# 128-column products set between longer ones, x put into PSUM ahead of the last product, and a new draw of the planner

## The chip, the cores and the metric

The kernel runs on one core of a Trainium2 chip. The time is device microseconds of that core for one execution of the whole block; the median of three runs before the change is 423.39 us (423.36 to 423.80). A profile of one execution stands beside it. The engines are named as in the profile: PE is TensorE (PEld its weight loads), DVE VectorE, ACT ScalarE, POOL GpSimd, SP the engine that issues most DMAs.

## The reference

One pre-norm residual layer over 512 tokens of width 1024, with two attention branches fed by one input projection. Its core, cut:

```python
h = rmsnorm(x, norm_g)
(q_lat, c_kv, k_rope, z_a, q_b, k_b, v_b, z_b,
 q_idx, k_idx, w_idx, gate_a, gate_b) = split(h @ w_in)
q  = rmsnorm(q_lat, g_q_lat) @ w_uq      # 8 heads of 64 + 32 (the 32 rotated)
kv = rmsnorm(c_kv, g_kv_lat) @ w_ukv     # 8 heads of 64 keys, 64 values
y_a = softmax_chunk_causal(q, k) @ v * silu(z_a)
# branch b: an indexer scores keys, each query keeps its top 128
y_b = softmax_topk(q_b k_b / 8 + rel_bias) @ v_b * silu(z_b)
merged = sigmoid(gate_a) * (y_a @ w_o_a) + sigmoid(gate_b) * (y_b @ w_o_b)
out = rmsnorm(x + merged @ w_out, final_g)
```

## The kernel before, in words

Nearly all of the work is matrix products. Each operand is kept as a rounded part ("hi", made by an ACT cast) and a remainder ("lo", made by a subtraction on DVE or POOL), and a product is summed in PSUM from two or three single products: hi*hi, hi*lo, lo*hi (`mm3`, `mm`, line 418). Tokens are four tiles of 128.

Order. Nothing is scheduled by the compiler: generators ("threads") yield steps, and a planner (`Flow.run`) keeps a clock for each engine, picks the step that can start first by its table of durations (with a random addition for each thread, from `random.Random(DRAW)`), and emits it. What it emits is the order of instructions on each engine's queue, and each engine runs its queue strictly in that order. `step` durations are the planner's own numbers, written in the code.

Logits. Each MLA head (`mla_head`) makes for token tile i a tile of logits of 128 (i + 1) columns, three products each (lines 1582 to 1584); each DSA head (`dsa_head`) two products each, through `mm`. `ORDER` lists the tiles, 0 to 3, each in its own PSUM bank. DVE takes a row maximum, ACT the exponential, the probabilities are normalised and turned by PE (line 435).

Attention outputs. `attend` multiplies values by the turned probabilities of the key tiles 0 to 3, of 512, 384, 256 and 128 columns, hi and lo, into one bank.

The loads of weights go through four raw buffers by `fetcher` on the SP queue. `PASSED` names four of them whose DMA is issued only after 2 or 6 later DMAs of that queue; one lo part of the DSA values is likewise emitted later than planned (`passed_by`).

The end (`output`). The output product is made of seven block products (numbers 1 to 7) with shared sums. Products 1, 7, 2, 6 and 5 come first; product 5 leaves its result in the banks z (one of 512 columns for the first tile, two of 256 for the second). Product 4 completes columns 0 to 511 of tiles 2 and 3, and product 3 adds to the banks z to complete columns 512 to 1023 of tiles 0 and 1. `finish` halves the bank and adds x on DVE (xr, line 357), takes the sum of squares (ACT Square, or for the very last piece a DVE reduction, line 1861) and multiplies by the gain into rg (line 357). `scale_out` adds the sums, takes the power on POOL (line 396), scales rg on DVE (line 376) or ACT (line 329) and stores it: seven DMAs on SP (line 458), one on ACT (line 1905).

Of the kernel before, what the change touches and what calls it, by code (L numbers as in the profile page):

```python
# [15 lines left out]
ALU = mybir.AluOpType  # L16
# [3 lines left out]
P = 128  # L20
# [243 lines left out]
DRAW = 53  # L264
# [6 lines left out]
def tile_block(ctx: ExitStack, tc: tile.TileContext, a: dict, out: bass.AP, bias_dram: bass.AP):  # L271
# [158 lines left out]
    def turn(parts):  # L430


        def emit():
            for d, s in parts:
                nc.tensor.transpose(d.ap, s.ap, ident.tile)  # L435

        return pe(0.107 * len(parts), [d for d, _ in parts], [s for _, s in parts] + [ident.all], emit, len(parts))

    held = []

    def hold(n, emit):

        return lambda: held.append([n, emit])

    def passed():
        for x in list(held):
            x[0] -= 1
            if not x[0]:
                held.remove(x)
                x[1]()  # L450

    def dma(dst, src):
# [5 lines left out]
        return Step([("SP", n / 360000.0, lambda: (nc.sync.dma_start(d, s), passed()))], bufs(dst), bufs(src))  # L458
# [494 lines left out]
    def fetcher():  # L953
        yield is_done("loads")
        for n, job in enumerate(jobs):
# [144 lines left out]
    passed_by = []  # L1100

    def seven(times, part, c11, c21, c12, c22, end):
# [11 lines left out]
        def add(dst, ps, y):  # L1114
            step = tt(dst, part(ps), y, ALU.add)
            return step.then(lambda: [passed_by.pop()() for _ in list(passed_by)])
# [32 lines left out]
    def values2():  # L1149
# [69 lines left out]
        def take(half, out):  # L1219
            v = yield Get(VV)  # L1220
            for u in range(2):
# [4 lines left out]
                step = lo_part(lo, src, hi)  # L1226
# [3 lines left out]
                yield step  # L1230
# [235 lines left out]
    def attend(br, h, probs, ready, prio):  # L1466
# [29 lines left out]
        for kt, pt, src, dst in ((0, 0, slice(0, S), slice(0, S)), (1, 1, slice(P, S), slice(P, S)),  # L1496
                                 (2, 2, slice(256, S), slice(256, S)), (3, 2, slice(P, 256), slice(384, S))):
            hi, lo = turned[pt]
            yield mm(ps[:, dst], [(v4[:, kt, :], hi[:, src]), (v4[:, kt, :], lo[:, src])], kt == 0, kt == 3)
            if kt != 2:  # L1500
                put(hi, lo)
# [51 lines left out]

    def mla_head(h):
# [7 lines left out]
        def soft(i, ps):  # L1562
            n = P * (i + 1)
            mx = yield Get(SMALL)
            yield Step([("DVE", 0.07 + 0.00104 * n, lambda: nc.vector.tensor_reduce(  # L1565
                mx.tile[:, 1:2], ps.tile[:, :n], op=ALU.max, axis=AX.X, negate=True))], [mx], [ps])
            den = yield from sums[i].at(i)
            yield act(probs[i], ps[:, :n], AF.Exp, bias=mx[:, 1:2], scale=1.0, accum=den)
            put(ps, mx)
            yield from sums[i].normalise(i, probs[i])  # L1570
            ready.add(i)

        for i in ORDER:
            nn = P * (i + 1)
            ps = yield bank("lg")

            def emit():
                o = ps.tile[:, :nn]
                q0, q1 = qh.tile[:, TOK[i]], ql.tile[:, TOK[i]]
                k0, k1 = kh.tile[:, :nn], kl.tile[:, :nn]  # L1580

                nc.tensor.matmul(o, q0[0:100], k0[0:100], start=True, stop=False)  # L1582
                nc.tensor.matmul(o, q0[0:96], k1[0:96], start=False, stop=False)  # L1583
                nc.tensor.matmul(o, q1[0:96], k0[0:96], start=False, stop=True)  # L1584

            yield pe(3 * (0.0133 + nn / 2400), [ps.all], [qh.all, ql.all, kh.all, kl.all], emit, 3)
            spawn(soft(i, ps), prio)
# [62 lines left out]
    def dsa_head(h):  # L1650
# [7 lines left out]
        def soft(i, ps):  # L1658
            n = P * (i + 1)
# [508 lines left out]
```

## Time and profile before

| what | value |
|---|---|
| median of three runs | 423.39 us |
| lowest, highest run | 423.36, 423.80 us |
| span of the profiled execution (first to last instruction) | 421.2 us |
| median less span | 2.19 us |
| granted TensorE clock, mean | 0.995 |
| PE, PEld busy | 413.7 us (98%), 364.3 us (86%) |
| DVE, ACT, POOL busy | 372.8 us (89%), 265.6 us (63%), 125.2 us (30%) |
| mean DMA rate | 156 GB/s |

The page lists no time of the profiled execution other than its span; the median less the span is what lies around the first and last instruction, as far as one execution and a median can be set against each other. A busy PE is not a PE at its peak, since ends of products are modelled; starts of products, starts of weight loads and the idle time before them tell more. Start and length of a row in the timeline are in us from the start of the span; "x7" merges seven instructions.

### The profile page before, as it was taken

The page shows a single profiled execution, that of the slowest core. Times are in us where ns is not written, and L with a number is a line of the kernel's source. Part 1 is how long each engine was busy: PE and PEld are TensorE (multiplying, and loading weights), DVE is VectorE, ACT ScalarE, POOL GpSimd, SP SyncE. Part 2 cuts the span into 40 slices and gives each one's busy share as a digit, 9 for nine tenths or more (in the row PEclk, how much of TensorE's full clock was granted, in tenths as well). Part 3 has the DMA queues.
Part 4 walks back from the last instruction along what each step waited for, and adds up shares of the span by engine and source line. Part 5 has one row for each costly group of instructions (what it writes and reads, how often), then busy time and mean ns, then how long its engine had stood idle before and what let it go on. Part 6 is the DMA issues. An engine that isn't in the chain of part 4 may idle for free.

```text
span 421.2 us, 7078 instructions
## 1 busy us (share of the span) xinstructions
PE 413.7 (98%) x2314; PEld 364.3 (86%) x2314; DVE 372.8 (89%) x797; ACT 265.6 (63%) x596; POOL 125.2 (30%) x139
## 2 busy tenths in 40 slices
PE   8999999999999999999999999999999999999994
PEld 7999878888888888888999988998998888888883
DVE  4879889569999999999999999979799768999995
ACT  5877778586754748625578677694597444336624
POOL 0047768543464669400012000200100000120652
PEclk9999999999999999999999999999999999999998
DMA  7992135665266441444652347144542887248305
GB/s 258 382 337 77 48 94 191 172 206 127 75 156 184 89 151 51 119 146 149 151 163 75 110 142 188 56 166 129 153 138 68 292 296 242 102 148 305 123 1 199
DMA packets 30645, 65.89 MB, mean 156 GB/s; under 512 B 4776, under 2 KB 6200, under 8 KB 30608
## 3 DMA queue, kind: packets, MB, share of 16 engines
q1 hardware_dynamic: 28256, 61.66, 47.4%
q10 hardware_dynamic: 1584, 2.62, 1.7%
q0 software_dynamic: 768, 1.15, 0.9%
q8 instruction: 18, 0.29, 0.3%
q14 instruction: 19, 0.16, 0.1%
HBM read 50.49 MB, written 4.21 MB: 130 GB/s over the span
## 4 chain that ended last, share of the span: by engine, by line
PE 96%; DVE 1%; DMA 1%; issue 0%; POOL 0%; ACT 0%; POOLq 0%; SPq 0%; ACTq 0%
PE ps L418 86%; PE ps L435 5%; PE ps L1583 1%; PE ps L1584 1%; PE ps L1582 1%; PE ps L883 1%; DMA normg<-norm_g 1%; DVE s_xr L357 1%; POOL sm L396 0%; DVE s_rg L357 0%; DVE s_rg L376 0%; ACT s_rg L329 0%; POOLq L2164 0%; ACT s_xg L329 0%; PE ps L932 0%
## 5 line engine op out<-in xcount | busy, mean ns | idle before, releaser
L418 PE MATMUL ps<-s_h,s_w 128*128 128x512 f32 (+1 forms) x732 | 169.9, 379 | 0.0
L418 PEld LDWEIGHTS ps<-s_h,s_w 128*128 128x128 f32 x732 | 128.3, 189 | 22.0
L320 ACT CAST s_w<-raw 128x512 fp32r<-128x512 f32 (+3 forms) x124 | 71.8, 593 | 18.8 <-DMA raw<-w_o 9.3
L348 POOL TENSOR_TENSOR s_w<-raw,s_w 128x512 fp32r<-128x512 f32 (+2 forms) x39 | 48.5, 1255 | 48.1 <-ACT s_w L320 44.2
L346 DVE TENSOR_TENSOR s_w<-raw,s_w 128x512 fp32r<-128x512 f32 (+2 forms) x85 | 55.7, 668 | 4.7 <-ACT s_w L320 3.7
L418 PE MATMUL ps<-s_ys,s_w 128*128 128x512 f32 x192 | 43.8, 389 | 0.0
L418 PEld LDWEIGHTS ps<-s_ys,s_w 128*128 128x128 f32 x192 | 36.0, 188 | 7.5
L329 ACT ACTIVATE s_p<-s_p,sm 128x128 f32<-128x128 f32 (+3 forms) x62 | 32.7, 550 | 5.0 <-DVE sm L1662 4.3
L418 PE MATMUL ps<-s_wo,s_mg 128*128 128x512 f32 (+1 forms) x156 | 33.2, 373 | 0.0
L418 PE MATMUL ps<-s_w,s_xg 128*128 128x328 f32 (+1 forms) x192 | 32.5, 323 | 0.0
L418 PEld LDWEIGHTS ps<-s_wo,s_mg 128*128 128x128 f32 x156 | 27.6, 188 | 5.2
L418 PEld LDWEIGHTS ps<-s_w,s_xg 128*128 128x128 f32 x192 | 31.4, 188 | 0.0
L346 DVE TENSOR_TENSOR s_ph<-ps,s_ph 128x384 fp32r<-128x384 f32 (+1 forms) x48 | 27.6, 593 | 1.0 <-ACT s_ph L320 0.7
L320 ACT CAST s_ph<-ps 128x384 fp32r<-128x384 f32 (+1 forms) x48 | 23.4, 515 | 6.4 <-PE ps L435 5.0
L329 ACT ACTIVATE s_p<-ps,sm 128x128 f32<-128x128 f32 (+3 forms) x32 | 16.8, 527 | 15.7 <-DVE sm L1565 15.6
L348 POOL TENSOR_TENSOR s_p<-s_bias,mask 128x128 f32<-128x128 f32 (+2 forms) x5 | 4.2, 854 | 74.0 <-DMA s_bias<-bias_scratch 39.6
L905 DVE MAX8 sm<-mask 128x8 f32<-128x384 f32 (+2 forms) x48 | 25.7, 549 | 0.2
L906 DVE MATCH_REPLACE8 mask<-sm,mask 128x384 f32<-128x384 f32 (+2 forms) x48 | 25.9, 541 | 0.0
L418 PE MATMUL ps<-s_ph,vv 128*128 128x512 f32 (+3 forms) x128 | 25.1, 318 | 0.0
L435 PE MATMUL ps<-ident,s_p 128*128 128x128 f32 x160 | 23.1, 273 | 0.0
L418 PEld LDWEIGHTS ps<-s_ph,vv 128*128 128x128 f32 x128 | 21.0, 188 | 2.4
L348 POOL TENSOR_TENSOR s_wo<-raw,s_wo 128x512 fp32r<-128x512 f32 x3 | 13.2, 4420 | 28.3 <-ACT s_wo L320 28.3
(194 smaller groups left out, 769.6 us busy)
## 6 DMA issues: line engine op xcount, KB each, us to landing
raw<-w_out SPq DMA_DIRECT2D x18, 512.0 KB, 3.3
s_op<-s_op SPq DMA_DIRECT2D x36, 128.0 KB, 2.3
raw<-w_ga SPq DMA_DIRECT2D x8, 512.0 KB
raw<-w_gb SPq DMA_DIRECT2D x8, 512.0 KB
raw<-w_o SPq DMA_DIRECT2D x16, 256.0 KB, 4.2
s_xn<-x SPq DMA_DIRECT2D x8, 256.0 KB, 4.8
bias_scratch<-s_sig ACTq DMA_DIRECT2D x8, 256.0 KB, 3.0
raw<-w_za SPq DMA_DIRECT2D x4, 512.0 KB, 4.7
```

What stands on the lines that cost most here:

```text
L320: nc.scalar.copy(dst.ap, src.ap)
L329: nc.scalar.activation(dst.ap, src.ap, func, **kw)
L346: opts.append(("DVE", 0.07 + 0.00104 * x.n, lambda: nc.vector.tensor_tensor(dst.ap, x.ap, y.ap, op=op)))
L348: opts.append(("POOL", 0.15 + 0.0021 * x.n, lambda: nc.gpsimd.tensor_tensor(dst.ap, x.ap, y.ap, op=op)))
L357: lambda: nc.vector.scalar_tensor_tensor(dst.ap, x.ap, sc(s), y.ap, op0=op0, op1=op1))],
L418: nc.tensor.matmul(ps.ap, l.ap, r.ap, start=start and i == 0, stop=stop and i == len(pairs) - 1, skip_group_check=more)
L435: nc.tensor.transpose(d.ap, s.ap, ident.tile)
L883: yield pe(0.005 + n / 2400, [ps.all], [qs[h].all, ks[0].all], lambda: nc.tensor.matmul(ps.tile[:, :n], qs[h].tile[:96, TOK[i]], ks[0].til ...
L905: yield Step([("DVE", t, lambda: nc.vector.max(m8.tile, work.tile))], [m8], [work])
L906: yield Step([("DVE", t, lambda: nc.vector.match_replace(work.tile, m8.tile, work.tile, MARK))], [work], [m8])
L1582: nc.tensor.matmul(o, q0[0:100], k0[0:100], start=True, stop=False)
L1583: nc.tensor.matmul(o, q0[0:96], k1[0:96], start=False, stop=False)
```

## The change

It has five parts. `ORDER` now groups token tiles: tiles 2 and 0 of a head share a PSUM bank (384 + 128 columns), and `logits` emits, for each of the two or three single products, first the one of 384 and then the one of 128 columns. `attend` puts the key tiles 1 (384 columns) and 3 (128) in one step, in turn, and leaves key tile 2 for last. The planner's duration of a product of 128 columns is 0.11 us behind another such, and by its columns otherwise (`spans`); a turn is 0.109 in place of 0.107. At the end, `add_first` adds 2x into the banks z on DVE before product 3, so that `finish_twice` squares (ACT) and scales (DVE) straight from PSUM; product 4 runs tile by tile; the outputs may be scaled on either engine, and the sums of squares have a buffer each. Last, `DRAW` is 64, and `PASSED` and `passed_by` are gone.

```diff
-DRAW = 53
+DRAW = 64
...
+    def spans(columns):
+        t, before = 0.0, S
+        for n in columns:
+            t += 0.11 if n <= P and before <= P else 0.0133 + n / 2400
+            before = n
+        return t
...
-        return pe(0.107 * len(parts), ...
+        return pe(0.109 * len(parts), ...
-    held = []
...
-            if n in PASSED:
-                step.options = [("SP", step.options[0][1], hold(PASSED[n], step.options[0][2]))]
...
-                if half == 1 and u == 0:
-                    step.options = [(e, t, lambda emit=emit: passed_by.append(emit)) for e, t, emit in step.options]
...
-        for kt, pt, src, dst in ((0, 0, slice(0, S), slice(0, S)), (1, 1, slice(P, S), slice(P, S)),
-                                 (2, 2, slice(256, S), slice(256, S)), (3, 2, slice(P, 256), slice(384, S))):
-            hi, lo = turned[pt]
-            yield mm(ps[:, dst], [(v4[:, kt, :], hi[:, src]), (v4[:, kt, :], lo[:, src])], kt == 0, kt == 3)
+        for kts in ((0,), (1, 3), (2,)):
+            seq = []
+            for c in range(2):
+                for kt in kts:
+                    pt, src, dst = parts[kt]
+                    seq.append((ps[:, dst], v4[:, kt, :], turned[pt][c][:, src]))
...
+    def logits(ps, rows, parts):
+        seq = []
+        for n, (q, k) in enumerate(parts):
+            for i in rows:
+                seq.append((logits_of(ps, rows, i), q(i), k(P * (i + 1)), n == 0 and i == rows[0], n == len(parts) - 1))
...
-        for i in ORDER:
+        for rows in ORDER:
             ps = yield bank("lg")
-            yield mm(ps[:, :nn], [(qb[:, TOK[i]], kh[:, :nn]), (qb[:, TOK[i]], kl[:, :nn])], True, True)
-            spawn(soft(i, ps), prio)
+            yield logits(ps, rows, [(lambda i: qb[:, TOK[i]], lambda nn, k=k: k[:, :nn]) for k in (kh, kl)])
+            release = shared(ps, rows)
+            for i in rows:
+                spawn(soft(i, logits_of(ps, rows, i), release), prio)
...
+    def add_first(t, half, c0, c1, ps):
+        r = xr[t, half].all.f[:, c0:c1]
+        yield stt(ps[:, c0:c1], r, 2.0, ps[:, c0:c1], ALU.mult, ALU.add)
+        done.add(("added", t, half, c0))
+    def finish_twice(t, half, c0, c1, ps, nth):
+        r = ps[:, c0:c1]
+        spawn(square(t, r, nth, 0.5), PSQUARE)
+        if (t, half) not in rg:
+            rg[t, half] = yield slot("rg")
+        yield stt(rg[t, half].all.f[:, c0:c1], r, 0.5 * D ** 0.5, fg[half].all.f[:, c0:c1], ALU.mult, ALU.mult)
+        done.add(("g", t, nth))
+        yield is_done(("sq", t, nth))
+        put(ps)
...
-        for half, engs in ((0, ("ACT",) if t == 0 else ("DVE",)), (1, ("ACT",))):
+        spawn(half_out(0, ("DVE",)), 0)
+        spawn(half_out(1, ("ACT",) if t == 1 else ("ACT", "DVE")), 0)
...
-        yield from product(4, v, left2, 256)
+        for i in range(2):
+            v.append((yield bank("o")))
+            for k in range(4):
+                yield mm3(v[i].all, cut(left2[k], ...), whole(right[4, k]), k == 0, k == 3)
...
-                yield is_done(("read", 2 + i, 1 + (c0 > 0)), ("sum", i, 1))
+                yield is_done(("added", i, 1, c0))
...
-ORDER = [0,1,2,3]
+ORDER = ((2, 0), (1,), (3,))
-PASSED = {7: 2, 8: 2, 9: 2, 10: 6}
```

How the instructions move. On PE, in the logits of one MLA head, before (qhi is the rounded query, s_op the other operands, ps the bank):

```order
L1582 MATMUL ps_98<-s_op_1286,qhi_74 128x128
L1583 MATMUL ps_98<-s_op_1310,qhi_74 128x128
L1584 MATMUL ps_98<-s_op_1286,s_op_1280 128x128
L1582 MATMUL ps_93<-s_op_1286,qhi_74 128x256
L1583 MATMUL ps_93<-s_op_1310,qhi_74 128x256
L1584 MATMUL ps_93<-s_op_1286,s_op_1280 128x256
```

and of the same head in the changed kernel:

```order
L1572 MATMUL ps_97<-s_op_1287,qhi_74 128x384
L1572 MATMUL ps_97<-s_op_1287,qhi_74 128x128
L1572 MATMUL ps_97<-s_op_1317,qhi_74 128x384
L1572 MATMUL ps_97<-s_op_1317,qhi_74 128x128
L1572 MATMUL ps_97<-s_op_1287,s_op_1278 128x384
L1572 MATMUL ps_97<-s_op_1287,s_op_1278 128x128
```

The three products of 128 columns stood in a row and now stand one by one behind those of 384. In the whole program 74 products other than turns have 128 columns; 41 of them followed another short one before, and 1 does now.

At the end, on DVE, the last rows before (s_xr is x plus what is summed so far, s_rg the output tile, sm and ssf the sums of squares; the brackets name whose work a row waits for):

```order
L357 SCALAR_TENSOR_TENSOR s_xr_4520<-ps_98,s_xr_4520 128x256 [waits PE_49]
L1861 ISA junk,sm_90<-s_xr_4520,sm_90 128x256 [waits DVE_49]
L1861 ISA sm_90 128x1
L357 SCALAR_TENSOR_TENSOR s_rg_4837<-s_xr_4520,s_fg_4538 128x256
L376 TENSOR_SCALAR s_rg_4664<-s_rg_4664,sm_90 128x512 [waits Pool_49]
```

and now:

```order
L357 SCALAR_TENSOR_TENSOR s_rg_4828<-ps_98,s_fg_4591 128x512 [waits Activation_49]
L376 TENSOR_SCALAR s_rg_4769<-s_rg_4769,sm_81 128x512
L365 TENSOR_SCALAR sm_89<-ssf_128,sm_89 128x1
L357 SCALAR_TENSOR_TENSOR s_rg_4848<-ps_92,s_fg_4591 128x256 [waits Activation_49]
L376 TENSOR_SCALAR s_rg_4664<-s_rg_4664,sm_89 128x512 [waits Pool_49]
L365 TENSOR_SCALAR sm_91<-ssf_130,ssf_131 128x1
L357 SCALAR_TENSOR_TENSOR s_rg_4848<-ps_94,s_fg_4591 128x256 [waits Activation_49]
L365 TENSOR_SCALAR sm_91<-ssf_132,sm_91 128x1 [waits DVE_49]
L376 TENSOR_SCALAR s_rg_4671<-s_rg_4671,sm_91 128x512 [waits Pool_49]
```

The addition of x and the DVE reduction are gone from the last piece; the gain is multiplied straight from the bank, and that row waits for ACT.

On ACT, the last rows of the changed kernel (ps_98 is tile 0, ps_92 and ps_94 are the halves of tile 1; sm_89 belongs to tile 0, sm_91 to tile 1):

```order
L329 ACTIVATE junk,ssf_128<-ps_98 128x512 [waits PE_49,Activation_49]
L329 ACTIVATE junk,ssf_131<-ps_92 128x256 [waits PE_49,Activation_49]
L329 ACTIVATE s_rg_4828<-s_rg_4828,sm_89 128x512 [waits Pool_49]
L329 ACTIVATE junk,ssf_132<-ps_94 128x256 [waits PE_49,Activation_49]
L329 ACTIVATE s_rg_4848<-s_rg_4848,sm_91 128x512 [waits Pool_49]
```

Three squares now read PSUM, and the scaling of tile 0 stands ahead of the last square.

More of the change, by code (lines that the diff above doesn't have):

```diff
@@ L435, in emit @@
                 nc.tensor.transpose(d.ap, s.ap, ident.tile)
-        return pe(0.107 * len(parts), [d for d, _ in parts], [s for _, s in parts] + [ident.all], emit, len(parts))
-    held = []
[L441 to L450, printed above, removed]
+        return pe(0.109 * len(parts), [d for d, _ in parts], [s for _, s in parts] + [ident.all], emit, len(parts))
     def dma(dst, src):
@@ L457, in dma @@
             n *= x
[L458 removed]
+        return Step([("SP", n / 360000.0, lambda: nc.sync.dma_start(d, s))], bufs(dst), bufs(src))
     def pool_dma(dst, src):
@@ L954, in fetcher @@
         yield is_done("loads")
-        for n, job in enumerate(jobs):
+        for job in jobs:
             raw = yield Get(RAW)
@@ L1114, in add @@
         def add(dst, ps, y):
-            step = tt(dst, part(ps), y, ALU.add)
-            return step.then(lambda: [passed_by.pop()() for _ in list(passed_by)])
+            return tt(dst, part(ps), y, ALU.add)
         x = yield bank("mm")
@@ L1552, in prob_tiles, with logits_of, shared, release @@
         return s, [v[0][:, 0:128], v[1][:, 0:256], v[0][:, 128:512], v[2]]
+    def logits_of(ps, rows, i):
+        c = sum(P * (r + 1) for r in rows if r < i)
+        return ps[:, c : c + P * (i + 1)]
+    def shared(ps, rows):
+        left = [len(rows)]
+        def release():
+            left[0] -= 1
+            if not left[0]:
+                put(ps)
+        return release
+    def logits(ps, rows, parts):
[3 more added lines that the diff above has]
+                seq.append((logits_of(ps, rows, i), q(i), k(P * (i + 1)), n == 0 and i == rows[0], n == len(parts) - 1))
+        def emit():
+            for o, q, k, start, stop in seq:
+                nc.tensor.matmul(o.ap, q.ap, k.ap, start=start, stop=stop, skip_group_check=len(rows) > 1)
+        return pe(spans(k.n for _, _, k, _, _ in seq), [ps.all],
+                  [v for _, q, k, _, _ in seq for v in (q, k)], emit, len(seq))
     def mla_head(h):
@@ L1845, in final_loads, with finish @@
         done.add("final")
-    ssf = [fixed(f"ssf{t}", [P, 4]) for t in range(NT)]
+    ssf = [[fixed(f"ssf{t}{n}", [P, 1]) for n in range(3)] for t in range(NT)]
     rg = {}
-    def finish(t, half, c0, c1, ps, nth, last, keep=False):
+    def finish(t, half, c0, c1, ps, nth, keep=False):
         r = xr[t, half].all.f[:, c0:c1]
@@ L1857, in finish @@
         done.add(("read", t, nth))
-        if last:
-            yield Until(lambda: t in partial_sum)
-            s = partial_sum[t]
-            step = Step([("DVE", 0.1 + 0.00104 * r.n, lambda: nc.vector.tensor_tensor_reduce(
-                junk.tile[:, : r.n], r.ap, r.ap, op0=ALU.mult, op1=ALU.add, scale=1.0, scalar=s.tile[:, 0:1],
-                accum_out=s.tile[:, 1:2]))], [junk, s], [r.buf, s])
-            step.count = 2
-            yield step
-            done.add(("sq", t, nth))
-            yield is_done(("sum", t))
-        else:
-            spawn(square(t, r, nth), PSQUARE)
+        spawn(square(t, r, nth), PSQUARE)
         if (t, half) not in rg:
@@ L1950, in output, with add_when_read @@
         for i in range(2):
-            spawn(finish(i, 0, 0, 512, x[i], 0, False), 0)
+            spawn(finish(i, 0, 0, 512, x[i], 0), 0)
         yield from get_banks(y)
         yield from product(6, y, left3, 0)
+        def add_when_read(i, c0, c1, ps):
+            yield is_done(("read", 2 + i, 1 + (c0 > 0)), ("sum", i, 1))
+            yield from add_first(i, 1, c0, c1, ps)
         def partial(i):
```

111 lines of the change are left out of this document (55 added, 56 removed).

## The prediction

> **What bounds the kernel now.** I read the engines' busy shares first, then the chain of waits, then the waits of PE and of its weight loads.
>
> ```profile
> span 421.2 us, 7078 instructions
> PE 413.7 (98%) x2314; PEld 364.3 (86%) x2314; DVE 372.8 (89%) x797; ACT 265.6 (63%) x596; POOL 125.2 (30%) x139
> PE 96%; DVE 1%; DMA 1%; issue 0%; POOL 0%; ACT 0%; POOLq 0%; SPq 0%; ACTq 0%
> PE ps L541 <- DVE neghalf L492: 1.1, 1, 1.1
> PEld ps L932 <- issue: 0.5, 2, 0.4
> PEld ps L418 <- DVE s_w L346: 0.4, 2, 0.3
> PEld ps L435 <- ACT s_tmp L320: 0.3, 1, 0.3
> PEld ps L883 <- DVE s_tmp L787: 0.2, 1, 0.2
> PEld ps L435 <- issue: 0.2, 1, 0.2
> ```
>
> The third row is the chain that ended last: 96% of it is PE. The first wait (line 541) is the start, before x is there. The five below it are all the waiting of weight loads that the trace lists (engine, line, what ended it; us, times, longest): 0.5 + 0.4 + 0.3 + 0.2 + 0.2 = 1.6 us of 421.2. So there are two places where time can be won: what the products themselves cost in a row, and the 6 us behind the last of them. Nothing that makes DVE or ACT lighter in the middle is worth more than those 1.6 us. The sum is made on the span of 421.2; the median of the runs shown is 423.39, 2.19 more, and I let that stay as it is. About 0.2% (0.85 us) is what a measurement of this kernel tells from no change.
>
> **Part 1, the products of 128 columns.** The change has the same 2311 products of the same shapes on PE, by its order, so only what a product costs behind another can differ. A long one's price, from three starts of groups:
>
> ```profile
> 177.50 26.75 PE L418 MATMUL ps<-s_h,s_w 128*128 128x512 f32 x117
> 204.09 3.04 PE L418 MATMUL ps<-s_w,s_h 128*128 128x256 f32 x24
> 206.96 3.04 PE L418 MATMUL ps<-s_w,s_hs 128*128 128x256 f32 x24
> ```
>
> (204.09 - 177.50) / 117 = 0.2273 us for 512 columns, (206.96 - 204.09) / 24 = 0.1196 for 256; on that line 384 columns cost 0.173 and 128 would cost 0.066. What a short one does cost, in a head of branch b (two of each length, 128 to 512):
>
> ```profile
> 243.57 1.44 PE L418 MATMUL ps<-s_op,qhi 128*128 128x128 f32 x8
> 244.84 3.58 PE L418 MATMUL ps<-s_h,s_w 128*128 128x512 f32 x15
> ```
>
> 244.84 - 243.57 = 1.27; less 2 x 0.2273, 2 x 0.173 and 2 x 0.1196 leaves 0.23, so 0.115 for each short one. One of the two stood behind a long product and one behind a short one; had the first cost 0.066, the total would have been 1.22. Why it doesn't, the weight loads show, here in a head of branch a:
>
> ```profile
> 104.98 0.23 PE L1582 MATMUL ps<-s_op,qhi 100*128 100x128 f32 x1
> 105.04 0.27 PE L1583 MATMUL ps<-s_op,qhi 96*128 96x128 f32 x1
> 105.15 0.28 PE L1584 MATMUL ps<-s_op,s_op 96*128 96x128 f32 x1
> 105.27 0.33 PE L1582 MATMUL ps<-s_op,qhi 100*128 100x256 f32 x1
> 105.44 0.28 PE L1583 MATMUL ps<-s_op,qhi 96*128 96x256 f32 x1
> 104.98 0.19 PEld L1583 LDWEIGHTS ps<-s_op,qhi 96*128 96x128 f32 x1
> 105.09 0.19 PEld L1584 LDWEIGHTS ps<-s_op,s_op 96*128 96x128 f32 x1
> 105.21 0.19 PEld L1582 LDWEIGHTS ps<-s_op,qhi 100*128 100x128 f32 x1
> ```
>
> The load for the second product starts at 104.98, when the first product starts, and the next two follow 0.11 and 0.12 later. So the queue of loads is one ahead: the load of product i+1 begins as product i starts, and takes 0.11. Where product i lasts longer than that, the load is hidden; where it lasts 0.066, product i+1 waits for its load, whatever it is itself and whatever stood before i. A lone short product therefore still makes the long one behind it start 0.11 after it: three pairs of 384 and 128 cost 3 x 0.173 + 3 x 0.115, as they do apart. (The second row starts 0.05 before its load can have ended, and the second product of 256 columns 0.17 behind the first instead of 0.12: the records shift 0.05 from one product to the next, and only sums over a group can be trusted.)
>
> By the order, 41 short products stood behind a short one and 1 does now. If a short one behind a long one did cost 0.066, the change would win 40 x (0.115 - 0.066) = 2.0 us. The bounds are -2.0 and 0; I take 0, since both the group's sum and the starts of the loads speak for it.
>
> [...]
>
> **Part 2, the order in the middle** (`attend` in three steps, `DRAW`, no `PASSED`). No instruction comes or goes on PE. What it can win is the 1.6 us above; what it can lose is the same kind of thing, an operand that comes late for PE, and DVE has little slack to make it good:
>
> ```profile
> DVE  4879889569999999999999999979799768999995
> ```
>
> (40 slices of 10.5 us, tenths busy.) A plan with another draw has other late operands; with five in this one, worth 0.2 to 0.5 each, I take as many in the next: 0, bounds -1.6 and +1.2 (below). That raw loads are no longer passed on SP's queue belongs here: it moves when weights land, and its cost would show as one of those waits.
>
> **Part 3, the end.** Product 3, the last 36 products, starts in both kernels behind the same amount of PE work.
>
> ```profile
> 409.11 5.80 PE L418 MATMUL ps<-s_wo,qhi 128*128 128x512 f32 x36
> 414.32 0.42 ACT L329 ACTIVATE junk<-s_xr 128x256 f32<-128x256 f32 x1
> 414.87 0.21 DVE L365 TENSOR_SCALAR sm<-ssf 128x1 f32<-128x1 f32 x1 [0.18 <-ACT junk L329]
> 415.00 0.41 DVE L357 SCALAR_TENSOR_TENSOR s_xr<-ps,s_xr 128x256 f32<-128x256 f32 x1
> 415.45 0.49 DVE L1861 CUSTOM_DVE_ANT_0 junk<-s_xr,sm 128x256 f32<-128x256 f32 x1
> 416.02 0.66 POOL L396 TENSOR_TENSOR sm<-sm,neghalf 128x1 f32<-128x1 f32 x1 [0.93 <-DVE sm L1861]
> 416.72 0.49 DVE L376 TENSOR_SCALAR s_rg<-s_rg,sm 128x512 f32<-128x512 f32 x1 [0.44 <-POOL sm L396]
> 417.47 0.34 ACTq L1905 DMA_DIRECT2D out<-s_rg  x1
> ```
>
> PE ends at 414.91. Before, the last piece goes: x added at 415.00, sum of squares at 415.45, power at 416.02, scaling at 416.72, store: 1.72 us from 415.00 to the scaling. Now, with x in the bank already, ACT squares from PSUM: 0.55 until DVE can use it (the same Square of 256 columns at 414.32, used at 414.87); the gain product reads the same bank and by the order waits for ACT: 0.41 (the row at 415.00 has its line and shape); the small sum 0.21; power and its hand-over 0.70 (416.02 to 416.72). That is 1.87: what the dropped add saves (0.45) is eaten by the gain product, now in series with the square. Term: +0.15; were the two side by side, it would be -0.26.
>
> [...]
>
> Ahead of the last Square on ACT's queue stands now the scaling of tile 0, which waits for that tile's power on POOL.
>
> ```profile
> 409.92 0.68 DVE L357 SCALAR_TENSOR_TENSOR s_rg<-s_xr,s_fg 128x512 f32<-128x512 f32 x1
> 413.00 0.63 ACT L329 ACTIVATE junk<-s_xr 128x512 f32<-128x512 f32 x1 [2.10 <-DVE s_xr L357]
> 413.62 0.71 ACT L329 ACTIVATE s_rg<-s_rg,sm 128x512 f32<-128x512 f32 x1
> ```
>
> Tile 0's bank is complete 12 x 0.2273 behind 409.11, at 411.84. Its Square (0.63, and 0.13 until DVE can use it, as for the small one), its gain product (0.68), a scaling of another tile that stands between on DVE (0.49), the small sum (0.21) and the power (0.70) make 2.84, so 414.68; with 0.71 for the scaling on ACT the last Square starts at 415.4 at best in place of 414.9: +0.5, or nothing if DVE can be that much quicker.
>
> In the other direction the stores: the last five left in a jam.
>
> ```profile
> 412.33 5.24 SPq L458 DMA_DIRECT2D out<-s_rg  x7
> GB/s 0 0 0 0 0 0 0 0 0 0 0 275 384 268 73 406 377 73 232 384 312 0 254 370 377 392 384 370 391 384 370 377 406 370 196 0 0 0 0 0
> ```
>
> (40 slices of 0.2825 us from 410.) From 416.2 to 419.8 the stores run at some 380 GB/s, 0.69 for each 256 KB, so the end is 5 stores from 416.2 and not the last issue at 417.47 plus one transfer. With the tiles' ends earlier by the saved adds, the last two would have the queue alone: some -0.4. I take +0.15 + 0.5 - 0.4, about **+0.3** for the end, bounds -0.3 (side by side, or no block on ACT, with the relief) and +0.9.
>
> The three adds of 2x cost nothing: they are hidden under product 4.
>
> ```profile
> 405.02 1.36 DVE L357 SCALAR_TENSOR_TENSOR s_xr<-ps,s_xr 128x256 f32<-128x256 f32 x3
> ```
>
> DVE ends the adds into xr that stand ahead of it at 406.38; three new ones of 0.68, 0.41 and 0.41 behind them end at 407.9, and product 3 wants the first at 409.11. Without that cover of 1.2 us they would cost 1.5 on PE.
>
> **Sum.** 423.39 + 0 + 0 + 0.3 = **423.7 us**, no measurable change.
>
> **The rivals.**
>
> S, slower: one operand is late at the end. POOL makes three remainders for the output product:
>
> ```profile
> 393.21 1.64 POOL L348 TENSOR_TENSOR s_wo<-s_wsum,s_wo 128x512 fp32r<-128x512 f32 x1 [18.23 <-ACT s_wo L320]
> 394.81 11.46 POOL L348 TENSOR_TENSOR s_wo<-raw,s_wo 128x512 fp32r<-128x512 f32 x2
> ```
>
> One took 1.64, the next two 5.73 each, beside a full DVE. In the new order the first POOL remainder is for product 5, which starts 24 x 0.2273 + 5.6 before 409.11, at 398.05; before, the first of the two slow ones belonged to product 4, wanted at 403.65. If it starts no earlier than the first did (393.21) and takes 5.73, it is ready at 398.94: PE stands 0.9, with the end's 0.3 423.39 + 1.2 = 424.6. It decides from a start after 392.3. Against it: POOL idles before 393.21, so it can begin as soon as its inputs are there.
>
> A, faster: the alternation pays, as worked out: 423.39 - 2.0 + 0.3 = 421.7. For it: the recorded start at 105.04 is 0.06 behind 104.98. Against it: the sum of 1.27 and the loads.
>
> D, faster: the new draw has no late operands and the five waits go: 423.39 - 1.6 + 0.3 = 422.1. For it: they are few and short. Against it: a full DVE leaves new ones.
>
> That x does not go in ahead of time (the adds late, product 3 waiting) is part of S in effect, +1.5 at most.
>
> **How the numbers follow.** Forecast 0.45 (its own range 423.0 to 424.3), S 0.24, A 0.17, D 0.14. The likeliest time is 423.7. For 8 in 10 the range takes in A and D's times and S: 421.6 to 425.2. Slower by over 0.2% is S and the forecast's upper edge: 0.21 + 0.04 = 0.25. Faster: A whole, most of D, and the lower edge: 0.17 + 0.11 + 0.02 = 0.30. The rest, 0.45, is within 0.2%.
>
> **What would show it.** Right, part 1: groups of 384 and 128 in turn take 3 x 0.173 + 3 x 0.115 = 0.86, and a load follows 0.11 behind the load of a lone short product; wrong: they take 0.72. Part 2: the waits of PEld sum to 1 to 2 us; wrong if one alone is above 0.6, above all at line 418 near 398, or if they are gone. Part 3: PE ends within 0.5 of 414.9, the last Square on ACT starts 0.5 or more behind it, the gain product waits for ACT, and the last store is issued at 417.5 to 418.3; wrong if the Square starts as PE ends. The whole is wrong if the span moves by over 0.85 with PE's end.

## The result, and the profile after

| | before | changed |
|---|---|---|
| median | 423.6 us (423.36 to 424.36, 4 runs) | 428.84 us (427.61 to 429.87, 4 runs) |
| ratio, 95% interval | | 1.0122 (1.0096 to 1.0147) |
| span of the profiled execution | 421.2 us | 425.8 us |
| start of product 3, the last 36 products | 409.11 | 413.31 |
| from there to the last instruction | 12.09 | 12.49 |

I forecast no change, 423.7 us, in a range of 421.6 to 425.2. The kernel is 5 us slower, outside of it. The four executions lie in two pairs, at 427.6 to 427.9 and 429.8 to 429.9; the profiled one is of the lower pair, and the upper one shows a lower mean clock (0.992 and 0.990 against 0.995), which is taken up below.

The page of the changed kernel: its span, its busy shares and the chain that ended last.

```profile
span 425.8 us, 7112 instructions
PE 415.8 (98%) x2314; PEld 364.9 (86%) x2314; DVE 374.7 (88%) x799; ACT 263.0 (62%) x592; POOL 131.5 (31%) x144
PE 81%; DVE 12%; issue 3%; ACT 3%; POOLq 0%; POOL 0%; DVEq 0%; ACTq 0%
```

The busy shares hardly tell the two kernels apart. The chain does: it was 96% PE, and now 12% of it runs through DVE. The waits of weight loads name the place (engine, line, what ended the wait; us, times, longest):

```profile
PEld ps L418 <- DVE mask L357: 1.7, 1, 1.7
PEld L536 <- DVE neghalf L487: 1.0, 1, 1.0
PEld ps L878 <- DVE mask L357: 1.0, 1, 1.0
PEld ps L878 <- DVE mask L365: 0.5, 1, 0.5
PEld ps L418 <- ACT s_xg L329: 0.4, 1, 0.4
PEld ps L418 <- DVE s_pair L346: 0.3, 1, 0.3
```

Three waits for `mask`, 3.2 us, are new. `mask` is where DVE sums the indexer's scores out of their PSUM banks; PE's next product into a bank waits for that read (0.53 and 1.49 us in the rows). Here is that stretch on the three engines, from the timeline:

```profile
67.84 0.39 PE L878 MATMUL ps<-s_qs,s_qs 96*128 96x512 f32 x1
68.76 0.39 PE L878 MATMUL ps<-s_qs,s_qs 96*128 96x256 f32 x1 [0.53 <-DVE mask L357]
70.64 1.65 PE L418 MATMUL ps<-s_lat,s_w 128*128 128x512 f32 x6 [1.49 <-DVE mask L357]
...
65.43 0.67 DVE L346 TENSOR_TENSOR s_tmp<-ps,ropec 128x512 f32<-128x512 f32 x1
66.02 2.16 DVE L346 TENSOR_TENSOR s_tmp<-s_tmp,ropes 128x512 f32<-128x512 f32 x1
68.10 0.60 DVE L357 SCALAR_TENSOR_TENSOR mask<-ps,widx,mask 128x384 f32<-128x384 f32 x1
69.26 0.67 DVE L346 TENSOR_TENSOR s_tmp<-ps,ropec 128x512 f32<-128x512 f32 x1
69.85 1.65 DVE L357 SCALAR_TENSOR_TENSOR mask<-ps,widx,mask 128x512 f32<-128x512 f32 x3
...
66.32 1.30 POOL L348 TENSOR_TENSOR s_w<-raw,s_w 128x512 fp32r<-128x512 f32 x1
```

One of the two rope products of 128 x 512 (`s_tmp` times `ropes`, both in SBUF) stands on DVE, ahead of the reads. It took 2.16 us where its twin with one operand in PSUM, one row above it, took 0.67: it ends at 68.18, after POOL's subtraction, which also works from SBUF, has ended at 67.62. The reads of the banks come at 68.10 and 69.85, and PE, which had run out of work at 68.23 and again at 69.15, starts at 68.76 and 70.64. Before, both rope products of this size were on POOL:

```profile
65.12 1.29 POOL L348 TENSOR_TENSOR s_tmp<-s_tmp,ropes 128x512 f32<-128x512 f32 x1
67.63 1.29 POOL L348 TENSOR_TENSOR s_tmp<-s_tmp,ropes 128x512 f32<-128x512 f32 x1
```

and DVE's reads were never late enough for PE to be listed as waiting. DVE's product (2.16) and POOL's subtraction (1.30) overlap, and the product ends 0.56 behind the subtraction, about what such a product takes alone (at most 0.70, below). That the two took turns is my estimate from these times; no row shows it, nor which of them came first, since DVE's is listed as starting 0.30 ahead. Operands in SBUF alone are not the cause. In the changed kernel's trace 161 of DVE's two-operand sums and products of 128 x 512 have both operands in SBUF and no POOL operation on tiles beside them, and none of these took over 0.70. Of 31 that overlap one, 7 took over 0.75, up to 2.29; two of 32 x 512 took 2.53 and 1.51 beside one. 18 of 128 x 512 with an operand in PSUM overlap one too, and none of them took over 0.70.

So of the 4.6 us in the span, 0.4 is the end, and 4.2 is gone before product 3 starts: 3.3 more listed waits (4.9 against 1.6, without the start), 0.2 from the first 27 us (the product that started at 27.58 starts at 27.77), and 0.7 that I place only in part (small waits near 234 to 245 us, of the kind `s_pair` and `s_xg`).

**The upper pair.** The changed kernel once more, profiled in an execution of 428.1 us, in windows of 2 us (columns: PE, PEld, DVE, ACT and POOL busy, then the granted clock, the DMA share and GB/s):

```profile
68.00:70.00 2.00, 1.16 (x5) 0.49 (x3) 2.00 (x5) 1.70 (x4) 0.18 (x2) 1.00 0.45 160
70.00:72.00 2.00, 0.80 (x3) 0.72 (x4) 2.00 (x5) 0.64 (x2) 2.00 (x2) 0.95 0.00 0
72.00:74.00 2.00, 2.00 (x7) 1.62 (x7) 2.00 (x4) 0.34 (x1) 1.98 (x3) 0.50 0.23 16
74.00:76.00 2.00, 2.00 (x14) 2.00 (x13) 2.00 (x3) 1.41 (x3) 0.40 (x1) 0.70 0.86 302
```

Behind the two pauses the granted clock falls to 0.50, and it comes back near 75.2. The first product behind this, in the profile shown first and in this one:

```profile
73.91 0.34 PE L878 MATMUL ps<-s_qs,s_qs 96*128 96x384 f32 x1
76.00 0.34 PE L878 MATMUL ps<-s_qs,s_qs 96*128 96x384 f32 x1
```

Product 3 starts at 415.40 in place of 413.31, and the same 2.09 us are lost by this row. But they are not all the clock's: this execution was 0.54 behind by the product of 27.77, which starts at 28.31 here, and 0.56 behind ahead of the pauses. The fall costs 2.09 - 0.56 = 1.5 us. Another profiled execution with these pauses and a fall (last Square first, below) gives 1.53 in the same way; a third (the holds with draw 64, below) has a mean clock of 0.94 from 60 to 90 us, as this one has, where the profile shown first has 1.00. So the pause is paid for twice, in a part of the executions: 2.7 us of waiting, and 1.5 us for the products at a clock of 0.50. What sets off the fall, and why only in a part of the executions, is not shown. PE was not idle for long at a time there: it was busy 1.96 of the 4 us from 68 to 72.

### The profile page after: what moved, and what is told of

Same layout as the page of the kernel before. It is cut to its first block, busy times and chain, and to the rows that moved or that the text cites. A ratio compares the mean times of both kernels' runs of the same rounds, so it can differ in the third digit from the quotient of the medians.

```text
span 425.8 us, 7112 instructions
## 1 busy us (share of the span) xinstructions
PE 415.8 (98%) x2314; PEld 364.9 (86%) x2314; DVE 374.7 (88%) x799; ACT 263.0 (62%) x592; POOL 131.5 (31%) x144
## 4 chain that ended last, share of the span: by engine, by line
PE 81%; DVE 12%; issue 3%; ACT 3%; POOLq 0%; POOL 0%; DVEq 0%; ACTq 0%
PE ps L418 65%; PE ps L1572 5%; PE ps L1492 5%; PE ps L443 4%; DVE s_tmp L346 2%; DVE s_tmp L357 2%; DVE s_w L346 1%; ACT junk L329 1%; PE ps L536 1%; DVE s_p L346 1%; DVE s_p L1676 1%; DVE s_h L346 1%; DVE raw L346 1%; DVE s_pair L346 1%; PE ps L878 1%
## 5 line engine op out<-in xcount | busy, mean ns | idle before, releaser
L348 POOL TENSOR_TENSOR s_w<-raw,s_w 128x512 fp32r<-128x512 f32 (+2 forms) x45 | 58.9, 1317 | 143.2 <-ACT s_w L320 124.0
L346 DVE TENSOR_TENSOR s_w<-raw,s_w 128x512 fp32r<-128x512 f32 (+3 forms) x79 | 50.6, 655 | 7.1 <-ACT s_w L320 6.7
L329 ACT ACTIVATE s_p<-s_p,sm 128x256 f32<-128x256 f32 (+3 forms) x58 | 30.5, 550 | 9.8 <-DVE sm L1676 9.7
L1572 PE MATMUL ps<-s_op,qhi 128*128 128x512 f32 (+11 forms) x128 | 26.4, 320 | 0.0
L1492 PE MATMUL ps<-s_ph,vv 128*128 128x512 f32 (+3 forms) x128 | 26.2, 325 | 0.0
L1572 PEld LDWEIGHTS ps<-s_op,qhi 128*128 128x128 f32 (+2 forms) x128 | 20.7, 189 | 2.2
```

The source lines that it names most:

```text
L329: nc.scalar.activation(dst.ap, src.ap, func, **kw)
L346: opts.append(("DVE", 0.07 + 0.00104 * x.n, lambda: nc.vector.tensor_tensor(dst.ap, x.ap, y.ap, op=op)))
L348: opts.append(("POOL", 0.15 + 0.0021 * x.n, lambda: nc.gpsimd.tensor_tensor(dst.ap, x.ap, y.ap, op=op)))
L1492: nc.tensor.matmul(o.ap, v.ap, p.ap, start=kts[0] == 0 and n == 0, stop=kts[0] == 2 and n == 1, skip_group_check=len(kts) > 1)
L1572: nc.tensor.matmul(o.ap, q.ap, k.ap, start=start, stop=stop, skip_group_check=len(rows) > 1)
```

## The experiments

All on chips with runs of the kernel before beside them. Times are medians; the ratio is to the kernel before.

| run | median us (lowest to highest) | ratio, 95% interval |
|---|---|---|
| changed, again | 429.53 (427.58 to 431.04) | 1.0125 (1.0097 to 1.0154) |
| rope products on POOL | 426.45 (426.04 to 426.82) | 1.006 (1.0041 to 1.0079) |
| pauses filled | 428.26 (427.54 to 429.95) | 1.0111 (1.0093 to 1.0129) |
| products apart | 428.87 (427.5 to 429.17) | 1.0114 (1.0091 to 1.0136) |
| last Square first | 429.43 (429.19 to 429.83) | 1.0133 (1.0112 to 1.0153) |
| before, new end only | 424.45 (423.73 to 424.99) | 1.0018 (1.0008 to 1.0029) |
| the same, scaling behind the Square | 423.79 (423.41 to 425.1) | 1.0011 (0.9999 to 1.0023) |
| before, draw 64 | 427.59 (427.56 to 428.11) | 1.0095 (1.008 to 1.0111) |
| changed, draw 53 | 429.87 (428.73 to 430.67) | 1.0144 (1.0123 to 1.0164) |
| changed, draw 53, holds | 427.99 (426.96 to 429.07) | 1.0102 (1.0081 to 1.0122) |
| changed, holds (draw 64) | 429.09 (427.58 to 429.6) | 1.0129 (1.0103 to 1.0154) |
| before, no holds | 424.79 (424.29 to 425.53) | 1.0031 (1.0021 to 1.0042) |
| before, grouped logits | 430.66 (427.91 to 431.78) | 1.0158 (1.013 to 1.0186) |
| before, draw 1 | 430.3 (429.91 to 431.46) | 1.0167 (1.0149 to 1.0186) |
| before, draw 2 | 429.89 (429.74 to 430.38) | 1.0155 (1.014 to 1.017) |
| changed, draw 1 | 434.2 (433.08 to 434.69) | 1.0251 (1.0232 to 1.0271) |

### What the pause is made of

**The changed kernel again**, for comparison on one chip.

> The changed kernel once more, beside the next three on one chip. Theory P (two waits of PE for the score banks between 67 and 71 us, 2.7 us, behind a rope product that DVE does in 2.16): the same two rows, span about 425.8, ratio 1.010 to 1.013. Theory C (the time is spread over many rows by the chip that it ran on): another span by more than 1 us, with the rows of waits unchanged.

It ran at 427.58, 427.60, 429.41, 429.66, 429.85 and 431.04, with the two waits of 1.7 and 1.0 as before and the clock at 0.998 in the first two and 0.990 to 0.991 in the others. Theory C falls: the same kernel on one chip does both.

**Rope products on POOL.** Only the engine that the product is issued to is changed; the plan, which thinks it on DVE, stays.

```diff
-        yield tt(sw.all.f[rows], sw.all.f[rows], ropes[rows], ALU.mult, BOTH)
+        step = tt(sw.all.f[rows], sw.all.f[rows], ropes[rows], ALU.mult, BOTH)
+        if rows == slice(0, P):
+            on_pool = step.options[1][2]
+            step.options = [(e, t, on_pool) for e, t, _ in step.options]
+        yield step
```

> The changed kernel with one thing other: the rope products with the sine (128 x 512, both operands in SBUF) are all issued to POOL; the plan and every other row stay as they are. In the changed kernel one of the three is on DVE, where it took 2.16 ahead of the reads of the score banks. Theory P: these reads come 1.4 to 2.2 us earlier, the waits of PE for mask (1.0 + 1.7) fall below 0.8 in all, the kernel is 1.9 to 2.7 us faster than the changed one, ratio to before 1.005 to 1.008. Rival Q (DVE is late as a whole by then, from the 2.53 and 1.51 rows at 52 to 59): the waits fall by a third at most, under 1 us. Rival L (what the scores need comes late by SP's queue, without the held loads): no change, under 0.3 us.

Its waits of weight loads:

```profile
PEld ps L882 <- DVE mask L357: 0.6, 1, 0.6
PEld ps L882 <- DVE s_op L357: 0.5, 1, 0.5
PEld ps L418 <- DVE mask L357: 0.5, 1, 0.5
PEld ps L882 <- DVE mask L365: 0.5, 1, 0.5
```

The waits for `mask` of 1.7 and 1.0 become 0.5 and 0.6: 1.1 in place of 2.7, where theory P had under 0.8 and rival Q nearly 2. Against the changed kernel's median it is 3.1 us faster, but most of this is the clock: no execution shows the fall, all six lie within 0.8 us. Against the changed kernel's executions without the fall (427.6) it is 1.2 us, less than the 1.9 expected; a wait of 0.5 for `s_op` is new. At the place itself PE is 2.07 us earlier (the product that started at 70.64 starts at 68.35, and this execution was 0.22 ahead before); 0.93 of this is lost again by 80 us. Rival L falls. The one product explains 1.6 of the 2.7 us of pause. Where the rest comes from is not shown; rival Q, that DVE is late as a whole by then, may hold for it.

**The pauses filled.** Useless products keep PE busy there.

```diff
+    AGAIN = {10: 3, 11: 12}          # repeats of the 10th and the 11th score product
...
-            yield pe(..., lambda: nc.tensor.matmul(ps.tile[:, :n], ..., start=True, stop=True))
+            def emit():
+                nth[0] += 1
+                for _ in range(1 + AGAIN.get(nth[0], 0)):
+                    nc.tensor.matmul(ps.tile[:, :n], ..., start=True, stop=True)
```

> The changed kernel with useless products in the two pauses of PE at 68 to 70.6 us: the score product ahead of the first pause is done 4 times over, the one between the pauses 13 times over, into their own banks with the same result; all else is the same. Theory G (the granted clock falls to 0.50 for some 3.4 us behind the pause in part of the executions, and that is the second half of the loss): no execution shows the fall, all have a clock of 0.995 or more and lie within 0.8 us of each other, 427.3 to 428.2, while the pauses' own 2.7 us stay. Rival R (the fall comes by itself, or from the chip): again about two of three executions at 428.7 or more with a clock under 0.995.

From 60 to 90 us, the changed kernel and then this one (columns as above):

```profile
60.00:90.00 30.00, 27.91 (x140) 23.22 (x139) 22.96 (x39) 18.94 (x43) 15.59 (x16) 1.00 0.66 180
```

```profile
60.00:90.00 30.00, 29.86 (x154) 25.21 (x154) 22.45 (x39) 19.29 (x43) 15.69 (x16) 1.00 0.63 179
```

PE is busy for 29.86 us in place of 27.91, and the kernel is not slower for it: 427.54, 427.87, 428.21, 428.31, 428.51 and 429.95. Of the executions of this change with its pauses left as they are (the changed kernel in its two series, products apart, last Square first, holds: 25) 18 were above 428.6, of the filled kernel 1 of 6, at a clock of 0.992. The numbers speak for theory G, but the one execution is not explained, and "no execution" was too much. It also shows why a busy share of PE is no measure of progress.

The runs suggest that the distance between the pauses counts, which none of them tests alone. The old code with draw 64 and with draw 2 (below) also pauses twice, 0.9 and 1.3 us and 0.9 and 1.5 us, but 8 to 9 us apart, and their eight executions have a clock of 0.995 to 0.998. A single pause of 3.4 us (before with grouped logits) or 3.6 us (before with draw 1) had the fall in the profiled execution, and in nine of ten executions a clock of 0.994 or less (kernels without such a pause come down to 0.994 too, so only the profiled ones are certain); here the latter, in windows of 4 us:

```profile
396.00:400.00 4.00, 2.04 (x10) 1.31 (x8) 3.90 (x7) 2.06 (x4) 0.74 (x1) 1.00 0.22 89
400.00:404.00 4.00, 2.36 (x5) 1.64 (x6) 3.69 (x5) 2.95 (x8) 0.80 (x1) 0.52 0.00 0
404.00:408.00 4.00, 4.00 (x17) 3.38 (x16) 3.94 (x6) 0.27 (x1) 1.67 (x1) 0.63 0.02 4
```

### The parts of the change

**Products apart.** The changed kernel, plan and steps as they are, with the products of one length in a row within a step again.

```diff
-            for o, q, k, start, stop in seq:
+            for o, q, k, start, stop in [x for i in range(len(rows)) for x in seq[i::len(rows)]]:
...
-                for n, (o, v, p) in enumerate(seq):
+                for n, (o, v, p) in enumerate([x for i in range(len(kts)) for x in seq[i::len(kts)]]):
```

> The changed kernel with the products of a step in the old order: within each step of logits and of attention outputs the products of one length stand in a row, then those of the other; plan, steps and all other rows are the same. My step on the weight loads (a short product makes the next load 0.11 long wherever it stands): the same time as the changed kernel within 0.4 us, and a group of three 384 and three 128 takes 0.86 either way. Rival A (a short one behind a long one costs 0.066): 1.5 to 2.0 us slower than the changed kernel, such a group 0.86 here and 0.72 there.

The same six products, first in turn (the changed kernel), then apart:

```profile
86.43 0.69 PE L1572 MATMUL ps<-s_op,qhi 100*128 100x384 f32 x4
86.95 0.45 PE L1572 MATMUL ps<-s_op,s_op 96*128 96x384 f32 x2
87.24 0.92 PE L418 MATMUL ps<-s_h,s_w 128*128 128x512 f32 x3
```

```profile
86.41 0.52 PE L1572 MATMUL ps<-s_op,qhi 100*128 100x384 f32 x2
...
87.11 0.28 PE L1572 MATMUL ps<-s_op,s_op 96*128 96x128 f32 x1
87.22 0.90 PE L418 MATMUL ps<-s_h,s_w 128*128 128x512 f32 x3
```

87.24 - 86.43 = 0.81 and 87.22 - 86.41 = 0.81. Taking turns is worth nothing: the two profiled executions, both without the fall, are within 0.1 us of each other still at the start of product 3 (413.31 and 413.39). Rival A falls. Less 3 x 0.173 for the long ones, 0.81 leaves 0.10 for each short one, as in the three that stand in a row in the kernel before (104.98 to 105.27).

**Last Square first.**

```diff
-        spawn(half_out(1, ("ACT",) if t == 1 else ("ACT", "DVE")), 0)
+        spawn(half_out(1, {0: ("DVE",), 1: ("ACT",)}.get(t, ("ACT", "DVE"))), 0)
```

> The changed kernel with the second half of tile 0 scaled on DVE in place of ACT, so that the last Square has no scaling ahead of it on ACT. My step on the end: the Square starts within 0.1 of PE's end instead of 0.47 behind it, the last store is issued 2.4 us behind PE's end instead of 2.91, and the kernel is 0.4 to 0.5 us faster than the changed one. Rival: the scaling (0.49) now stands ahead of the last gain product on DVE, or the stores set the end: less than 0.15 us.

The Square starts at 420.83, 0.09 behind PE's end at 420.74 (product 3 starts at 414.94 and takes 5.80), but the last store is issued 2.87 behind PE's end, 0.04 better than the changed kernel's 2.91. The rival holds:

```profile
420.83 0.38 ACT L329 ACTIVATE junk<-ps 128x256 f32<-128x256 f32 x1 [0.94 <-PE ps L418]
421.27 0.48 DVE L376 TENSOR_SCALAR s_rg<-s_rg,sm 128x512 f32<-128x512 f32 x1
421.66 0.42 DVE L357 SCALAR_TENSOR_TENSOR s_rg<-ps,s_fg 128x256 f32<-128x256 f32 x1
```

The scaling of tile 0 now stands ahead of the last gain product instead of ahead of the last Square.

**Before, with the new end only**, all of the end's code and nothing else.

> The kernel before with the new end only (x into the banks ahead of product 3, product 4 tile by tile, Square and gain product from PSUM); what comes ahead of the output product is the same. My step on the end: 12.5 us from the start of product 3 to the last instruction in place of 12.09, so +0.3 to +0.5 us, ratio 1.0007 to 1.0012. Rival: the remainders of product 5 on POOL are late and PE stands 0.6 or more near 398: +1.0 or more.

424.45, 1.1 above the kernel before beside it (0.8 by the ratio), more than I had expected, but not by the rival: no wait near 398. Product 3 starts at 409.84 and the last instruction ends 13.26 later (12.09 before). In this plan the power of tile 0 is later, and ACT waits for it ahead of the last Square:

```profile
415.68 0.55 POOL L396 TENSOR_TENSOR sm<-sm,neghalf 128x1 f32<-128x1 f32 x1 [1.72 <-DVE sm L365]
416.26 0.72 ACT L329 ACTIVATE s_rg<-s_rg,sm 128x512 f32<-128x512 f32 x1 [1.46 <-POOL sm L396]
416.89 0.36 ACT L329 ACTIVATE junk<-ps 128x256 f32<-128x256 f32 x1
419.33 0.34 ACTq L1907 DMA_DIRECT2D out<-s_rg  x1
```

The Square starts 1.25 behind PE's end at 415.64.

**The same, with that scaling behind the last Square.**

```diff
         def half_out(half, engs):
+            if t == 0 and half == 1:
+                yield is_done(("sq", 1, 2))
...
-        spawn(half_out(1, ("ACT",) if t == 1 else ("ACT", "DVE")), 0)
+        spawn(half_out(1, ("ACT",) if t < 2 else ("ACT", "DVE")), 0)
```

> The kernel before with the new end only, as in the run end_only, but the scaling of tile 0 on ACT emitted behind the last Square. My step on ACT's queue: the last Square starts within 0.1 of PE's end instead of 1.25 behind it, the last store is issued about 2.45 behind PE's end, and the kernel is 1.0 us or more faster than end_only: 423.2 to 423.7, the same as before within 0.2%. Rival: the stores set the end, and it is less than 0.4 faster than end_only.

The Square starts at 415.39, 0.09 behind PE's end; the store is issued 3.26 behind it, not 2.45, because on DVE the other scaling of tile 0 waits for the same late power (416.08) and the last gain product stands behind it (416.61). It lies 0.52 above its runs of the kernel before, where the run with the new end only lay 1.08 above its own: 0.56 us faster by the medians, 0.3 by the ratios, whose intervals overlap. In the traces the end is 0.36 shorter (12.90 from the start of product 3 in place of 13.26), and 0.34 of the difference lies ahead of product 3, where nothing was changed. So the gain is some 0.4, and my step, 1.0 or more, failed; whether it is less than the 0.4 of the rival can't be told. The kernel is not to be told from the one before. The rows suggest that the power of tile 0 is late and that whichever engine holds its scalings passes this on.

### The plan

**Before, with draw 64**, one number changed.

```diff
-DRAW = 53
+DRAW = 64
```

> The kernel before with the new draw, 64, and nothing else (by its order one rope product of 128 x 512 is on DVE, as in the changed kernel). Theory D: a wait of PE for mask of 1 us or more near 65 to 71 us, 425.5 to 430 with executions on both sides of a fall of the clock. Rival S: 423 to 424.3, no such wait.

427.59: the old code, with the new draw, loses 4.2 us. Its waits:

```profile
PEld ps L883 <- DVE mask L357: 1.7, 1, 1.7
PEld ps L418 <- DVE mask L357: 1.3, 1, 1.3
```

The rope product is on DVE here too, at 66.67, and takes 2.28. By this pair of kernels theory D holds, but for the fall of the clock, which none of the four executions shows (0.995 to 0.996).

**The changed kernel with draw 53** (the same edit the other way round).

> The changed kernel with the old draw, 53: all of the change but that number (by its order no rope product of 128 x 512 is on DVE). Theory D (the draw alone brought the stall): no wait of PE for mask above 0.5 us, no fall of the clock, start of product 3 near 409.5, plus 0.4 for the end: 423.8 to 425.0. Rival S (the grouped logits or the missing holds on SP's queue bring it): 426.5 or more with waits for mask again.

429.87, and there theory D, as I had put it, falls: no rope product on DVE, no wait for `mask`, and still 6 us lost, most of it in small waits for other things.

```profile
PEld ps L418 <- DVE s_w L346: 1.7, 4, 0.8
PEld ps L443 <- ACT s_p L329: 1.0, 2, 0.7
PEld ps L878 <- DVE vv L346: 0.8, 1, 0.8
```

Of the listed waits 3.3 us lie between 222 and 237, and the end takes 13.9 us from the start of product 3 in place of 12.09. So it is not "the draw" alone. Four runs ask whether the missing holds or the grouped logits are to blame.

**Before, without the holds** (`PASSED` and `passed_by` have no effect; plan as it is).

```diff
-            if n in PASSED:
+            if False:
...
-                if half == 1 and u == 0:
+                if False:
```

> The kernel before without its two holds: the four raw loads and the one remainder of the values are issued where the plan has them; the plan and every other row stay. Theory H (the holds are what the changed kernel lacks, on any plan): PE waits for s_w near 30 to 60 us or near 222 to 237 us appear, 0.8 to 2.5 us in all, ratio 1.002 to 1.006. Theory D (each plan has late operands of its own, the holds mend little): under 0.5 us, ratio below 1.001.

+1.5 us (424.79), with a wait of 1.1 for `mask` at 78 us and one of 0.3 for `s_pair`. On the old plan the holds are worth that. Theory H had the size, but neither the operand nor the place: it named `s_w`, near 30 to 60 or 222 to 237.

**The changed kernel with draw 53 and the holds back.**

> The changed kernel with draw 53 and both holds back, otherwise as the run with draw 53 (429.87, of which some 3.5 us were lost near 222 to 237 us). Theory H: the loss near 222 to 237 falls below 1 us, 425 to 427. Theory D: it stays, 428.5 to 431.

427.99, 1.9 us faster than without, but the waits for `s_w` stay (1.4 us, 3 times) and 2.5 us of waits are still listed between 222 and 237. Neither theory; the holds explain a part.

**The changed kernel, draw 64, with the holds back.**

> The changed kernel with draw 64 and both holds back, so that only the emission of four raw loads and one remainder differs from the changed kernel. Theory H (as on the old plan, where leaving them out cost 1.5 us): 0.8 to 2 us faster than the changed kernel. Theory D (the holds were fitted to the old plan alone): within 0.7 us of the changed kernel, the waits for mask at 67 to 71 us as they were.

427.58 to 429.6, as the changed kernel itself, with the waits of 1.7 and 0.9 for `mask`; one wait for `s_pair` is gone. On this plan the holds do nothing that can be measured.

**Before, with the grouped logits and attention outputs only**, draw 53, holds, old end.

> The kernel before with the grouped logits and attention outputs only (two tiles in one bank, products of 384 and 128 in turn, the planner's price of a short product), with draw 53, the holds and the old end. Theory D (any other plan has late operands, since 53 had been picked for the old one): 1 to 4 us slower, with new waits for s_w, s_p or mask. Rival N (the grouping leaves the plan as good): within 0.8 us. Rival A (the turn-taking pays): 1 to 2 us faster.

430.66, the worst of the single parts, above all by one long wait:

```profile
PEld ps L418 <- DVE s_wo L346: 3.7, 1, 3.7
```

A remainder of the output weights is 3.7 us late near 404. This is the pause that my rival S had described, at the output product, in another kernel than the one it was meant for; and the clock falls behind it. With draw 53, the grouping alone thus costs more than the whole change with the holds (427.99). The parts do not add up: each edit makes another order.

**Two draws taken without looking.** The old code with draws 1 and 2, the new one with draw 1.

> The kernel before with draw 1, taken without looking, and nothing else changed. Theory D (the plan of draw 53 with its holds is a good one among many; another order has late operands, whatever the code): 425 to 431, with waits of PE of 2 us or more in all. Rival X (the old code is good by itself): within 1 us of 423.4.

> The kernel before with draw 2, the same question as with draw 1. Theory D: 425 to 431; rival X: within 1 us of 423.4.

> The changed kernel with draw 1. Theory D: 425 to 431, on either side of the old code with the same draw. Rival X (the new code is worse by itself): at least 2 us above the old code with the same draw.

430.3, 429.89 and 434.2. The old code loses 6 to 7 us with either, once by one wait for `s_wo` of 4.0, once by two for `mask` (1.9 and 1.3) and some ten small ones. With draw 2 a rope product is on DVE again, by the order of its instructions; with draw 1 none is. So the three plans with a rope product on DVE (either code with draw 64, the old one with draw 2) are those with two long waits for `mask`. The new code with draw 1 lies 4 above the old one with the same draw. For the old code rival X falls: it is not good by itself, it is good with draw 53 and the holds. For the new one the single pair speaks for X (4 us), draw 53 too (428.0 with the holds against 423.4), draw 64 hardly (428.8 against 427.6, and 427.6 too in the new code's executions without the fall). Whether the new code is worse on the average over draws stays open with three pairs.

No run was faster than the kernel before.

## Why the prediction was wrong

**Part 1 was right.** Turn-taking is worth 0: 0.81 either way, where I had worked out 0.86 for the six and 0.72 for rival A. A short product's price of 0.115 was a little high, 0.10. The page lists 2314 products in both kernels where I wrote 2311, which changes nothing.

**Part 2 is the step that failed**: "I take as many in the next: 0, bounds -1.6 and +1.2". Measured: PE reaches product 3 4.2 us later, with 3.3 us more of listed waits, and 1.5 later again where the clock fell. The error has two halves. I took the size of a wait, 0.2 to 0.5, from the waits of one plan, and this plan is a good one: with two draws taken blind the same code waits for 4.0, or for 1.9 and 1.3, at once. The trace of a picked plan says nothing on how late an operand is in another. And I looked for late operands only at the output product (rival S), by the rows of POOL there, when the order of instructions of the changed kernel already showed one rope product moved from POOL to DVE, ahead of the reads of the score banks. The price was to be had, too: in the trace of the kernel before, two of DVE's additions from SBUF, at 68.61, took 2.69 together, where a row of this size with a PSUM operand takes 0.68, with POOL at work beside them.

**Part 3** came to +0.4 where I had +0.3, by a wrong sum: that the number is close is luck. Right: the Square 0.47 behind PE's end (0.5), the gain product in series behind it. The changed kernel's rows:

```profile
418.95 0.72 ACT L329 ACTIVATE s_rg<-s_rg,sm 128x512 f32<-128x512 f32 x1 [0.69 <-POOL sm L396]
419.58 0.36 ACT L329 ACTIVATE junk<-ps 128x256 f32<-128x256 f32 x1
420.07 0.42 DVE L357 SCALAR_TENSOR_TENSOR s_rg<-ps,s_fg 128x256 f32<-128x256 f32 x1 [0.51 <-ACT junk L329]
422.02 0.34 ACTq L1922 DMA_DIRECT2D out<-s_rg  x1
```

Wrong: the relief of 0.4 at the stores. The last store is issued 2.91 behind PE's end in place of 2.56, and from there it is 3.78 us to the end, 3.73 before. So the last issue sets the end, not the jam of stores; in six other traces it is 3.66 to 3.85 from there. And the two terms that were left came to +0.35 and not +0.65: from the Square to the scaling it is 1.69 (419.58 to 421.27), where I had worked out 1.87. And the term is one of the plan as well: 12.49 with draw 64, 13.26 with the old order ahead of it. The cover of the additions of 2x held: no run but the new code with draw 1 has PE wait for them (1.2 us there).

**The rivals.** S had the kind right, an operand late for PE that makes it slower, and its 424.6 was too near: place, price and the second payment by the clock were all other. That the clock could fall was nowhere in my sum; it adds 1.5 us to the 2.7 us of pause, in most of the executions. A and D fell. "The whole is wrong if the span moves by over 0.85 with PE's end" is what happened.

## What to carry to other kernels

Where a planner sets the order, its random draw and hand-made holds can be worth more than the edits: 4 to 7 us between draws of one code here, against 0 for the products, 0.4 to 1.1 for the end. So a change that makes a new plan should be judged against several draws of the old code, and its forecast should read the new order for steps that went to another engine ahead of the reads that PE waits for. A pause of PE can cost more than its own length: two of 0.5 and 1.5 us within 2.4 us cost 1.5 us on top in two profiled executions.

## What the runs showed of the hardware

- Behind two pauses of PE of 0.5 and 1.5 us within 2.4 us the granted clock fell to 0.50 and cost 1.5 us in two profiled executions, for 3.4 us by their windows; by their times 18 of 25 executions had the fall. With one pause of 3.6 us (old code, draw 1) the clock was 0.52 and 0.63 in the windows from 400 to 408 us, 6.8 us at 0.50 by my estimate from these. Two pauses of 0.9 and 1.3 to 1.5 us that lie 8 to 9 us apart had no fall in two profiled executions, and none of their eight has a clock under 0.995.
- A DVE product of 128 x 512 with both operands in SBUF took 2.16 us (changed kernel) and 2.28 (old code, draw 64) beside a POOL operation on SBUF. In the changed kernel's trace such sums and products took at most 0.70 with no POOL operation on tiles beside them (161) or with one operand in PSUM; with both in SBUF and such an operation beside them, 7 of 31 took over 0.75.
- A product of 128 columns cost 0.10 us in turn with longer ones and apart (six products, three of them of 384 at 0.173, took 0.81 us either way), where the line through 512 and 256 columns gives an estimate of 0.066.
